# A hybrid decoder layer in fp32: where the DMAs that prepare a first sum of weights stand in the queue, and how they are laid out

## The chip, the cores and the metric

The kernel runs on one core of one Trainium2 chip. The metric is the device time of one execution in microseconds (us). Nothing else runs on the core's 16 DMA engines. Bytes that pass through HBM scratch cost nothing by themselves; only the time of the whole execution counts.

## The reference

One layer works on 256 tokens of width 4096, all in float32:

```
u     = rmsnorm(x) * norm_gain
proj  = u @ w_in                       # 4096 -> 16384: q k v z_a | h B C z_c
attn  = causal attention of 16 heads x 128, T5 bias, times silu(z_a)
conv  = B * short_conv(C * h) * silu(z_c)
out   = rmsnorm(x + concat(attn, conv) @ w_out) * final_gain     # 4096 -> 4096
```

With 256 tokens there is one attention block, so the block selection selects nothing and plain causal attention is left. Nearly all work is in the two projections: 4096x16384 and 4096x4096 weights, read once each, against 256 tokens.

## The kernel before

**Products.** TensorE multiplies in fp32r, which keeps less than fp32. So each operand is split in two, a rounded part `hi` and the rest `lo`, and a product is three matmuls: token-hi by weight-hi (line 644), token-lo by weight-hi (L645) and token-hi by weight-lo (L647). Each matmul is 128x128 by 128x512.

**Quads.** The weights are worked off in 320 *quads*. A quad holds 2 row blocks of 128 by 2 column blocks of 512 of a weight matrix, as one 128x2048 array (1 MB). Sixteen quads are one *pass*: a pair of column blocks over all 4096 rows. There are 16 passes of the input projection (`w`) and 4 of the output projection (`wout`). A quad is multiplied with the two token halves in one of two ways. A plain quad (P) takes eight products, 24 matmuls. A *seven* (S) takes Strassen's scheme in Winograd's form, seven products, 21 matmuls; it needs sums of its four weight blocks first. A string such as `"PSPSSPSSPSSPSSPP"` (`PATS`) fixes the order of P and S in a pass.

**Work on a quad's weights.** `load(n)` fetches quad n into one of three SBUF buffers `raw` (`AHEAD + 1`); it is called two quads ahead. `split(u)` then makes the operands. For a seven, VectorE (DVE) makes three blocks `sum`: one from `raw` (L552) and two more at once (L553). ScalarE (ACT) rounds `hi` (L570), VectorE subtracts for `lo` (L572). `hi` and `lo` have three buffers each (`RING`), and a seven takes two of them in turn, one for its four raw blocks and one for its three sums. A raw buffer is free when the last `lo` of its quad has been made, and the load of the quad three further on can then be issued.

**The first sum.** The first of a seven's sums, of blocks 12 and 11 of the quad, is not made on VectorE but by DMA, for the 150 sevens from pass 2 on (the list `PRE`). `first_sum(n)` copies block 12 of quad n (256 KB, the first 512 columns of the 128x2048 array) from HBM to a scratch place in HBM, with a DMA on the queue of SyncE (SP, L493), and then adds the second 512 columns to it by an accumulating DMA on the queue of GpSimd (POOL, L494). When the quad is loaded, its first 512 columns come from the scratch place (L515) and the other 1536 from the weights (L516). A quad outside `PRE` is loaded by one DMA (L518). The scratch is one tile of four places (`T1S`), used in turn. `load(n)` calls `first_sum` for a later seven, as long as fewer than three first sums are ahead, so that the k-th seven's load is written together with the copy for seven k+3.

**Order.** Each engine and each queue works off its instructions strictly in order, and the SP queue holds the raw loads, the copies, and small transfers (attention bias, intermediate results, tokens). A framework builds the order: it takes the kernel as written, works out which instruction depends on which, and may place an instruction that depends on less ahead of one that was written earlier. So the copies of `first_sum` need not stand where `load` writes them. An instruction at the head of a queue that waits holds up everything behind it. The copy for a place in scratch must wait until the last read of that place (an L515) has landed.

Of the kernel before, what the change touches and what calls it, by code (L numbers as in the profile page):

```python
# [10 lines left out]
F32 = mybir.dt.float32  # L11
# [3 lines left out]
ALU = mybir.AluOpType  # L15
AX = mybir.AxisListType

P = 128
# [3 lines left out]
NQ = KT // 2  # L22
# [6 lines left out]
B = 512  # L29
QUAD = 4 * B  # L30
WARM = 10
PRE_FROM = 2
T1S = 4
T1_AT = 26
AHEAD = 2

# [32 lines left out]
N_PAIRS = 16  # L69
# [11 lines left out]
def of(pattern):  # L81
    n = pattern.count("S")
    return in_order(pattern, SEVEN[:n], EIGHT + SEVEN[n:]), set(SEVEN[:n])
# [3 lines left out]
ORDERS, SEVENS = zip(*([(FIRST0, {8, 10, 12, 14}), (SECOND, {4, 6, 8, 10, 12, 14})]  # L87
                       + [of(PATS[k]) for k in KIND[2:N_PAIRS]]
                       + [(FIRST, {8, 10, 12, 14})] + [of(PATS[k]) for k in KIND[N_PAIRS + 1:]]))

BOTH = {q for q in range(NQ) for a, b in ((0, N_PAIRS), (N_PAIRS, N_PAIRS + NDP)) for p in range(a, b)
        if q in SEVENS[p] and any(q not in SEVENS[x] for x in range(p, b))}
SIZES = [8 if q in BOTH else 7 if any(q in x for x in SEVENS) else 4 for q in range(NQ)]

RAISE = {(1, 1): 4, (1, 3): 6, (1, 6): 0, (1, 8): 2, (1, 10): 11,
         (N_PAIRS, 6): 0, (N_PAIRS, 8): 2, (N_PAIRS, 10): 4, (N_PAIRS, 12): 6}
# [7 lines left out]
def hymba_layer(ctx: ExitStack, tc: tile.TileContext, xT, xres, gain, w, convw, wout,  # L104
                relb, onehot, fgain, out):
    nc = tc.nc
    PSUM = bass.MemoryType.PSUM
    ps_ = ctx.enter_context(tc.tile_pool(name="ps", bufs=1, space=PSUM))
    dram = ctx.enter_context(tc.tile_pool(name="dram", bufs=1, space=bass.MemoryType.DRAM))
# [42 lines left out]
    def operands(q):  # L152
        A[q] = kt.tile([P, SIZES[q], 2, P], F32R, name=f"k{q}")
        return A[q]

    def sums_of(q, c):

        for dst, a, b, op in ((4, 0, 2, ALU.add), (5, 4, 1, ALU.subtract),
                              (6, 3, 5, ALU.subtract), (g_at(q), 0, 1, ALU.subtract)):
            nc.vector.tensor_tensor(c[:, dst], c[:, a], c[:, b], op)  # L160

    def parts(dst, c):
        nc.scalar.copy(dst[:, :, 0], c)  # L163
        nc.vector.tensor_tensor(dst[:, :, 1], c, dst[:, :, 0].bitcast(F32), ALU.subtract)  # L164

    def x_load(q):
        xr = pool.tile([P, 2, S], F32, name="xr", tag="pt", bufs=4)
        nc.sync.dma_start(xr, xT[q].rearrange("p (k t) -> p k t", k=2))
        return xr
# [8 lines left out]
    def x_parts(q, xr):  # L178
        dst = operands(q)
        if q in SEVENS[0]:  # L180
            c = x_scaled(q, xr)
            sums_of(q, c)
            parts(dst, c[:, :SIZES[q]])
            return
# [12 lines left out]
    def m_parts(q, c):  # L197
        dst = operands(q)
        if q in SEVENS[N_PAIRS]:
            sums_of(q, c)  # L200
            parts(dst, c[:, :SIZES[q]])
        else:
# [275 lines left out]
            nc.sync.dma_start(out[t * P:(t + 1) * P, a:b], row)  # L478


    quads = [(p, i, q) for p, order in enumerate(ORDERS) for i, q in enumerate(order)]
    raws, xrs, halves, sums, kept_at = {}, {}, {}, {}, []

    PRE = [n for n, (p, i, q) in enumerate(quads) if q in SEVENS[p] and p >= PRE_FROM]
    t1_d = dram.tile([T1S, P, B], F32, name="t1_d")
    t1s, t1_next = {}, [0]

    def source(n):
        return w[n] if n < w.shape[0] else wout[n - w.shape[0]]

    def first_sum(n):
        t1 = t1s[n] = t1_d[PRE.index(n) % T1S]
        nc.sync.dma_start(t1, source(n)[:, :B])  # L493
        nc.gpsimd.dma_start(t1, source(n)[:, B:2 * B], accum_op=ALU.add)  # L494

    def load(n):
        if n >= len(quads):
            return
        p, i, q = quads[n]
        raw = raws[n] = wp.tile([P, QUAD], F32, name="raw", bufs=AHEAD + 1)  # L500
        src = source(n)
        if p == 0:
            if i == 0:
                nc.scalar.dma_start(g_sb, gain)
                xr = xrs[q] = pool.tile([P, 2, S], F32, name="xr", tag="pt", bufs=4)
                nc.scalar.dma_start(xr[:, 1], xT[q][:, S:])
            else:
                xrs[q] = x_load(q)
        if n < LEAD:
            for j in range(4):  # L510
                nc.sync.dma_start(raw[:, j * B:(j + 1) * B], src[:, j * B:(j + 1) * B])
                if n == 0 and j == 0:
                    nc.sync.dma_start(xrs[q][:, 0], xT[q][:, :S])
        elif n in PRE:
            nc.sync.dma_start(raw[:, :B], t1s.pop(n))  # L515
            nc.sync.dma_start(raw[:, B:], src[:, B:])  # L516
        else:
            nc.sync.dma_start(raw, src)  # L518
        if n >= T1_AT and len(t1s) < T1S - 1 and t1_next[0] < len(PRE):
            first_sum(PRE[t1_next[0]])  # L520
            t1_next[0] += 1


# [12 lines left out]
    def split(u):  # L536
# [4 lines left out]
        if first:  # L541
            load(n + AHEAD)
            if p == 0:
                x_parts(q, xrs.pop(q))
            if q in SEVENS[p]:
                raw = raws[n].rearrange("p (b c) -> p b c", b=4)

                k = sum(x in SEVENS[p] for x in ORDERS[p][:i])
                t = sums[n] = (cur["pool"] if k % 2 and p < N_PAIRS else wp).tile([P, 3, B], F32, name="sum")
                if n not in PRE:  # L550
                    nc.vector.tensor_tensor(raw[:, 0], raw[:, 0], raw[:, 1], ALU.add)
                nc.vector.tensor_tensor(t[:, 0], raw[:, 0], raw[:, 2], ALU.subtract)  # L552
                nc.vector.tensor_tensor(t[:, 1:], raw[:, 1::2], t[:, :1].to_broadcast([P, 2, B]), ALU.subtract)  # L553
# [3 lines left out]
        if p == N_PAIRS + NDP - 1 and i >= KEPT:  # L557

            spot = ORDERS[p][2 * len(kept_at):]
            kept_at.append(u)  # L560
            hi, lo = (kt.tile([P, SIZES[k], 2, P], F32R, name=f"k{k}")
                      .rearrange("p n h c -> p (n h c)") for k in spot[:2])
# [60 lines left out]
    for n in range(AHEAD):  # L623
        load(n)
# [25 lines left out]
    for u, (n, kind, at, products) in enumerate(units):  # L650
        p, i, q = quads[n]
# [16 lines left out]
        g = AHEAD_HI if len(products) > 2 and not late else 1  # L668
# [43 lines left out]
        if (p, i + 1) in RAISE:  # L712
            q = RAISE[p, i + 1]
            raised[q] = x_load(q) if p < N_PAIRS else m_load(q)
        if (p, i) in RAISE:
            q = RAISE[p, i]
# [21 lines left out]


def _layout(x, norm_gain, w_in, conv_w, w_out, rel_bias, final_gain):  # L740
    def blocks(src, order, c1, c2):

        b1, b2 = src[:, :, c1:c1 + B], src[:, :, c2:c2 + B]
        return [np.concatenate((b2[2 * q], b1[2 * q], b2[2 * q + 1], b1[2 * q + 1]), axis=1) for q in order]

    w = w_in[0].reshape(KT, P, 4 * 4096)
    w_quads = []
    for p, ((c1, c2), g) in enumerate(PAIRS):
        w_quads += blocks(w, ORDERS[p], c1 * 2048 + g * B, c2 * 2048 + g * B)
    w_quads = np.stack(w_quads)  # L750
    wo = w_out[0].reshape(KT, P, D)
    wo_quads = []
    for p in range(NDP):
        wo_quads += blocks(wo, ORDERS[N_PAIRS + p], 2 * p * B, (2 * p + 1) * B)
    wo_quads = np.stack(wo_quads)

    dist = 255 - np.arange(384)
    bucket = np.where(dist < 0, BUCKETS,
                      np.where(dist < 16, dist, 15 + np.searchsorted(EDGES, dist, side="right")))
    onehot = (bucket[None, :] == np.arange(BUCKETS + 1)[:, None]).astype(np.float32)  # L760
    return {
        "xT": x[0].T.reshape(NQ, 2, P, S).transpose(0, 2, 1, 3).reshape(NQ, P, 2 * S),
        "xres": x[0].reshape(2, P, NDP, 2 * B).transpose(2, 1, 0, 3).reshape(NDP, P, 4 * B),
        "gain": norm_gain[0].reshape(KT, P).T,
        "w": w_quads,
        "convw": conv_w[0].reshape(3, 16, P).transpose(2, 1, 0),
        "wout": wo_quads,
        "relb": rel_bias,
        "onehot": onehot,
        "fgain": final_gain,  # L770
    }
# [22 lines left out]
```

## Time and profile before

| | |
|---|---|
| median of 3 runs | 1818.78 us (1814.21 to 1820.96) |
| profiled execution | 1825.3 us, of which the span of the profile is 1823.5 us |
| TensorE busy in the profile | 1727.6 us, 95% of the span |
| VectorE busy | 1502.6 us, 82% |
| ScalarE busy | 1049.6 us, 58% |
| mean granted TensorE clock | 0.980 |
| moved by DMA | 449.21 MB, 246 GB/s over the span |

Busy times count an instruction from its start to its modelled end, and matmuls overlap each other: one is shown as 396 ns long, though in an undisturbed stretch they start every 0.227 us. So a busy share of TensorE of 95% does not say that 5% is all that is lost. A row of the timeline gives start, duration, engine, line, operation and what it writes and reads; a "q" behind the engine's name (SPq) means its queue, and the time of a DMA's row there is only that of issuing it. Brackets behind a row hold how long the engine had been idle and what it had waited for.

### The profile page before, as it was taken

To read this page: it belongs to the slowest core of one execution; us is meant where nothing else is said; L and a number is where in the kernel's file an instruction comes from. 1 tells how busy PE (TensorE), PEld (TensorE's weight loads), DVE (VectorE), ACT (ScalarE), POOL (GpSimd) and SP (SyncE) were. 2 spreads that over 40 slices of the span, in tenths; PEclk is the share of its full clock that TensorE was granted. 3 is DMA by queue.
4 is the path that set the end of the run, shared out by engine and by line. 5 is a ranking of instruction groups with operands and counts; after the bars stand their busy time and mean duration, and the time that the engine had idled before them with its cause. 6 is when DMAs were issued, how large, how long until landed. Compare 5 with 4: busy or idle time off the path is not lost.

```text
span 1823.5 us, 20698 instructions
## 1 busy us (share of the span) xinstructions
PE 1727.6 (95%) x7580; PEld 1408.4 (77%) x7580; DVE 1502.6 (82%) x1286; ACT 1049.6 (58%) x1161; POOL 124.2 (7%) x156
## 2 busy tenths in 40 slices
PE   9999999999999998989999999999999999999997
PEld 7888777777778777868777887787778777778776
DVE  6989787878797878878797978887889877878787
ACT  6867655665566555655465555555555645555453
POOL 0000100010000000000000000000000000000000
PEclk9999999999999999999999999999999999999998
DMA  9877877888787878687888888878888879787864
GB/s 335 282 264 246 238 255 225 254 239 257 205 271 220 261 216 263 178 247 231 240 258 251 259 244 241 272 209 254 232 268 237 285 262 300 233 256 225 249 222 168
DMA packets 131505, 449.21 MB, mean 246 GB/s; under 512 B 16171, under 2 KB 21068, under 8 KB 109900
## 3 DMA queue, kind: packets, MB, share of 16 engines
q1 hardware_dynamic: 109516, 408.42, 64.3%
q0 software_dynamic: 21600, 39.33, 15.3%
q8 instruction: 59, 0.97, 0.2%
q14 instruction: 42, 0.34, 0.1%
q10 hardware_dynamic: 288, 0.15, 0.0%
HBM read 438.66 MB, written 87.82 MB: 289 GB/s over the span
## 4 chain that ended last, share of the span: by engine, by line
PE 42%; DMA 28%; DVE 19%; issue 8%; ACT 2%; SPq 1%; DVEq 0%; ACTq 0%
DMA raw<-in_w_dram 17%; PE p L647 14%; PE p L645 13%; PE p L644 13%; DVE lo L572 13%; DMA raw<-in_wout_dram 6%; DMA raw<-t_d 2%; DVE sum L552 2%; ACT hi L570 2%; DVE sum L553 1%; DMA m_d<-mt 1%; SPq L515 1%; DMA c<-m_d 1%; PE p L283 0%; DMA xr<-in_xT_dram 0%
## 5 line engine op out<-in xcount | busy, mean ns | idle before, releaser
L644 PE MATMUL p<-hi,k 128*128 128x512 f32 x2376 | 937.1, 396 | 10.9 <-DVE es L375 4.1
L645 PE MATMUL p<-hi,k 128*128 128x512 f32 x2376 | 935.3, 395 | 0.1
L570 ACT CAST hi<-raw 128x1024 fp32r<-128x1024 f32 (+1 forms) x638 | 638.0, 1044 | 442.6 <-PE p L645 256.7
L572 DVE TENSOR_TENSOR lo<-raw,hi 128x2048 fp32r<-128x2048 f32 (+1 forms) x323 | 723.5, 2247 | 73.4 <-ACT hi L570 72.7
L647 PE MATMUL p<-lo,k 128*128 128x512 f32 x2376 | 648.0, 396 | 66.1 <-DVE lo L572 66.0
L647 PEld LDWEIGHTS p<-lo,k 128*128 128x128 f32 x2376 | 443.3, 189 | 169.0 <-DVE lo L572 82.1
L644 PEld LDWEIGHTS p<-hi,k 128*128 128x128 f32 x2376 | 454.2, 191 | 111.2 <-ACT hi L570 8.3
L645 PEld LDWEIGHTS p<-hi,k 128*128 128x128 f32 x2376 | 453.4, 191 | 96.9 <-issue 0.6
L570 ACT CAST hi<-sum 128x1536 fp32r<-128x1536 f32 x160 | 237.0, 1482 | 218.1 <-PE p L645 90.2
L572 DVE TENSOR_TENSOR lo<-sum,hi 128x1536 fp32r<-128x1536 f32 x160 | 280.3, 1752 | 9.6 <-ACT hi L570 8.8
L552 DVE TENSOR_TENSOR sum<-raw 128x512 f32<-128x512 f32 x160 | 110.1, 688 | 197.6 <-DMA raw<-in_w_dram 156.3
L553 DVE TENSOR_TENSOR sum<-raw,sum 128x1024 f32<-128x1024 f32 x160 | 195.5, 1222 | 2.7
L494 POOL DMA_DIRECT2D t_d<-in_w_dram x125 | 103.0, 830 | 1289.7 <-DMA t_d<-in_w_dram 1288.3
L382 ACT ACTIVATE es<-es,rT 128x512 f32<-128x512 f32 x56 | 38.3, 718 | 26.2 <-DVE es L376 20.9
L494 POOL DMA_DIRECT2D t_d<-in_wout_dram x25 | 20.5, 820 | 336.4 <-DMA t_d<-in_wout_dram 336.4
L163 ACT CAST k<-c 128x512 fp32r<-128x512 f32 (+4 forms) x38 | 21.8, 591 | 35.6 <-DVE c L160 24.4
L164 DVE TENSOR_TENSOR k<-c,k 128x512 fp32r<-128x512 f32 (+4 forms) x38 | 24.0, 650 | 0.7 <-ACT k L163 0.6
L160 DVE TENSOR_TENSOR c<-c 128x128 f32<-128x128 f32 x68 | 17.0, 286 | 9.0 <-DMA c<-m_d 7.9
L376 DVE TENSOR_TENSOR es<-p,es 128x1024 f32<-128x1024 f32 x20 | 24.3, 1217 | 0.0
L291 ACT ACTIVATE lg<-lg,st 128x256 f32<-128x256 f32 (+1 forms) x32 | 14.3, 447 | 6.2 <-DVE st L290 6.2
L283 PE MATMUL p<-qk 128*128 128x256 f32 x32 | 11.2, 436 | 4.9 <-ACT qk L278 4.0
L361 DVE SCALAR_TENSOR_TENSOR y<-p,cw,y 128x255 f32<-128x255 f32 (+1 forms) x32 | 14.1, 474 | 0.1
(107 smaller groups left out, 479.5 us busy)
## 6 DMA issues: line engine op xcount, KB each, us to landing
raw<-in_w_dram SPq DMA_DIRECT2D x129, 1024.0 KB, 7.1
raw<-in_w_dram SPq DMA_DIRECT2D x125, 768.0 KB, 6.9
raw<-in_wout_dram SPq DMA_DIRECT2D x39, 1024.0 KB, 7.4
raw<-t_d SPq DMA_DIRECT2D x150, 256.0 KB, 5.2
t_d<-in_w_dram SPq DMA_DIRECT2D x125, 256.0 KB, 5.3
t_d<-in_w_dram POOLq DMA_DIRECT2D x125, 256.0 KB, 7.1
raw<-in_wout_dram SPq DMA_DIRECT2D x25, 768.0 KB, 6.2
t_d<-in_wout_dram SPq DMA_DIRECT2D x25, 256.0 KB, 5.7
```

The costliest lines, as they stand in the source:

```text
L163: nc.scalar.copy(dst[:, :, 0], c)
L164: nc.vector.tensor_tensor(dst[:, :, 1], c, dst[:, :, 0].bitcast(F32), ALU.subtract)
L376: nc.vector.tensor_tensor(es[:, 1::2], acc[5][:, None, :].to_broadcast([P, 2, B]), es[:, 1:3], ALU.subtract)
L382: nc.scalar.activation(e, e, AF.Copy, scale=r)
L494: nc.gpsimd.dma_start(t1, source(n)[:, B:2 * B], accum_op=ALU.add)
L552: nc.vector.tensor_tensor(t[:, 0], raw[:, 0], raw[:, 2], ALU.subtract)
L553: nc.vector.tensor_tensor(t[:, 1:], raw[:, 1::2], t[:, :1].to_broadcast([P, 2, B]), ALU.subtract)
L570: nc.scalar.copy(hi[:, b:b + half], src[:, b:b + half])
L572: nc.vector.tensor_tensor(lo[:, c], src[:, c], hi[:, c].bitcast(F32), ALU.subtract)
L644: nc.tensor.matmul(acc[b_], a, h_, start=s0, stop=False)
L645: nc.tensor.matmul(acc[b_], b, h_, start=False, stop=False)
L647: nc.tensor.matmul(acc[b_], a, l_, start=False, stop=s1)
```

## The change

The change has four parts.

- The scratch has eight places instead of four, each a tile of its own. The number of first sums in the making stays at three (`T1_LEAD`).
- The call of `first_sum` in `load` is wrapped so that its SP instruction, the copy, must stand in the SP queue behind the last DMA of the raw load that it is written with.
- For the 150 sevens of `PRE`, the host lays out block 12 as 256 KB in one piece, and behind it the other three blocks as 128 rows of 6 KB. Before, all four were 128 rows of 8 KB. Bytes, and the shapes in SBUF, are the same.
- The copy of block 12 is now from one contiguous region to another, written as 32 pieces of 8 KB (`COPY`). The built instruction has 16 rows of 16 KB. Before it had 128 rows of 2 KB. The accumulating DMA and the load from scratch still go by 128 rows of 2 KB.

What is computed, on which engine, and the number of DMAs stay as they were.

```
-T1S = 4
+T1S = 8
+T1_LEAD = 3
+COPY = 32
...
+QUADS = [(p, i, q) for p, order in enumerate(ORDERS) for i, q in enumerate(order)]
+
+PRE = [n for n, (p, i, q) in enumerate(QUADS) if q in SEVENS[p] and p >= PRE_FROM]
...
-    t1_d = dram.tile([T1S, P, B], F32, name="t1_d")
+    t1_d = [dram.tile([COPY, P * B // COPY], F32, name=f"t1_{j}") for j in range(T1S)]
     t1s, t1_next = {}, [0]
...
+    def parted(n):
+
+        flat = source(n).rearrange("p c -> (p c)")
+        return flat[:P * B].rearrange("(a c) -> a c", a=COPY), flat[P * B:].rearrange("(p c) -> p c", p=P)
+
+    def by_rows(t1):
+        return t1.rearrange("a (r c) -> (a r) c", c=B)
+
     def first_sum(n):
         t1 = t1s[n] = t1_d[PRE.index(n) % T1S]
-        nc.sync.dma_start(t1, source(n)[:, :B])
-        nc.gpsimd.dma_start(t1, source(n)[:, B:2 * B], accum_op=ALU.add)
+        b12, rest = parted(n)
+        nc.sync.dma_start(t1, b12)
+        nc.gpsimd.dma_start(by_rows(t1), rest[:, :B], accum_op=ALU.add)
...
         elif n in PRE:
-            nc.sync.dma_start(raw[:, :B], t1s.pop(n))
-            nc.sync.dma_start(raw[:, B:], src[:, B:])
+            nc.sync.dma_start(raw[:, :B], by_rows(t1s.pop(n)))
+            last = nc.sync.dma_start(raw[:, B:], parted(n)[1])
         else:
-            nc.sync.dma_start(raw, src)
-        if n >= T1_AT and len(t1s) < T1S - 1 and t1_next[0] < len(PRE):
-            first_sum(PRE[t1_next[0]])
+            last = nc.sync.dma_start(raw, src)
+        if n >= T1_AT and len(t1s) < T1_LEAD and t1_next[0] < len(PRE):
+
+            with tc.issue_after(last.ins):
+                first_sum(PRE[t1_next[0]])
             t1_next[0] += 1
...
-        return [np.concatenate((b2[2 * q], b1[2 * q], b2[2 * q + 1], b1[2 * q + 1]), axis=1) for q in order]
+        made = []
+        for i, q in enumerate(ORDERS[p]):
+            first, rest = b2[2 * q], np.concatenate((b1[2 * q], b2[2 * q + 1], b1[2 * q + 1]), axis=1)
+            if NQ * p + i in PRE:
+                made.append(np.concatenate((first.reshape(-1), rest.reshape(-1))).reshape(P, QUAD))
+            else:
+                made.append(np.concatenate((first, rest), axis=1))
+        return made
```

How this moves the SP queue shows at two places. The first is in pass 2, where the order of the copies first departs from the written one. In these rows `raw<-t_d` (L515) and `raw<-in_w_dram` with 1536 columns (L516) are a seven's load, `raw<-in_w_dram` with 2048 columns (L518) is a plain quad's, and `t_d<-in_w_dram` (L493) is a copy. Before, two sevens, a plain quad and two sevens:

```order
L515 DMA raw<-t_d 128x512
L516 DMA raw<-in_w_dram 128x1536
L493 DMA t_d<-in_w_dram 128x512
L518 DMA raw<-in_w_dram 128x2048
L493 DMA t_d<-in_w_dram 128x512
L515 DMA raw<-t_d 128x512
L516 DMA raw<-in_w_dram 128x1536
L493 DMA t_d<-in_w_dram 128x512
L515 DMA raw<-t_d 128x512
L516 DMA raw<-in_w_dram 128x1536
L493 DMA t_d<-in_w_dram 128x512
```

The same place with the change; the lines are now L527 and L528 for a seven's load, L530 for a plain quad's and L505 for the copy, and the places in scratch are `t_0` to `t_7`:

```order
L527 DMA raw<-t_4_108 128x512
L528 DMA raw<-in_w_dram 128x1536
L505 DMA t_7_111<-in_w_dram 16x4096
L530 DMA raw<-in_w_dram 128x2048
L527 DMA raw<-t_5_109 128x512
L528 DMA raw<-in_w_dram 128x1536
L505 DMA t_0_104<-in_w_dram 16x4096
L527 DMA raw<-t_6_110 128x512
L528 DMA raw<-in_w_dram 128x1536
L505 DMA t_1_105<-in_w_dram 16x4096
```

Before, a second copy stands between the plain quad's load and the seven's load that it is written with. From there on the queue before is one copy ahead: what follows the load of seven k is the copy for seven k+4, and its place, k+4 modulo 4, is the very place that the load of seven k has just begun to read. With the change the copy that follows the load of seven k is for seven k+3, and its place was last read by the load of seven k-5.

The second place is where pass 2 ends and pass 3 begins. Before, three plain loads in a row, then two sevens' loads with a plain one between them:

```order
L518 DMA raw<-in_w_dram 128x2048 x3
L515 DMA raw<-t_d 128x512
L516 DMA raw<-in_w_dram 128x1536
L518 DMA raw<-in_w_dram 128x2048
L515 DMA raw<-t_d 128x512
L516 DMA raw<-in_w_dram 128x1536
L493 DMA t_d<-in_w_dram 128x512 x2
L515 DMA raw<-t_d 128x512
```

With the change:

```order
L530 DMA raw<-in_w_dram 128x2048 x3
L527 DMA raw<-t_1_105 128x512
L528 DMA raw<-in_w_dram 128x1536
L505 DMA t_4_108<-in_w_dram 16x4096
L530 DMA raw<-in_w_dram 128x2048
L527 DMA raw<-t_2_106 128x512
L528 DMA raw<-in_w_dram 128x1536
L505 DMA t_5_109<-in_w_dram 16x4096
```

Here two copies stood together ahead of a seven's load; now each stands behind a load, the first of them ahead of a plain quad's load instead. The order on GpSimd's queue, one accumulating DMA behind the other, is unchanged.

More of the change, by code (lines that the diff above doesn't have):

```diff
@@ L478, in finish @@
             nc.sync.dma_start(out[t * P:(t + 1) * P, a:b], row)
-    quads = [(p, i, q) for p, order in enumerate(ORDERS) for i, q in enumerate(order)]
+    quads = QUADS
     raws, xrs, halves, sums, kept_at = {}, {}, {}, {}, []
-    PRE = [n for n, (p, i, q) in enumerate(quads) if q in SEVENS[p] and p >= PRE_FROM]
-    t1_d = dram.tile([T1S, P, B], F32, name="t1_d")
+    t1_d = [dram.tile([COPY, P * B // COPY], F32, name=f"t1_{j}") for j in range(T1S)]
     t1s, t1_next = {}, [0]
@@ L740, in _layout, with blocks @@
 def _layout(x, norm_gain, w_in, conv_w, w_out, rel_bias, final_gain):
-    def blocks(src, order, c1, c2):
+    def blocks(src, p, c1, c2):
         b1, b2 = src[:, :, c1:c1 + B], src[:, :, c2:c2 + B]
-        return [np.concatenate((b2[2 * q], b1[2 * q], b2[2 * q + 1], b1[2 * q + 1]), axis=1) for q in order]
+        made = []
[6 more added lines that the diff above has]
+        return made
     w = w_in[0].reshape(KT, P, 4 * 4096)
@@ L748, in _layout @@
     for p, ((c1, c2), g) in enumerate(PAIRS):
-        w_quads += blocks(w, ORDERS[p], c1 * 2048 + g * B, c2 * 2048 + g * B)
+        w_quads += blocks(w, p, c1 * 2048 + g * B, c2 * 2048 + g * B)
     w_quads = np.stack(w_quads)
@@ L753, in _layout @@
     for p in range(NDP):
-        wo_quads += blocks(wo, ORDERS[N_PAIRS + p], 2 * p * B, (2 * p + 1) * B)
+        wo_quads += blocks(wo, N_PAIRS + p, 2 * p * B, (2 * p + 1) * B)
     wo_quads = np.stack(wo_quads)
```

## The prediction

> **What bounds the kernel now.** First the page: the span, busy times, DMA, and the chain that ended last.
>
> ```profile
> span 1823.5 us, 20698 instructions
> PE 1727.6 (95%) x7580; PEld 1408.4 (77%) x7580; DVE 1502.6 (82%) x1286; ACT 1049.6 (58%) x1161; POOL 124.2 (7%) x156
> DMA  9877877888787878687888888878888879787864
> q1 hardware_dynamic: 109516, 408.42, 64.3%
> q0 software_dynamic: 21600, 39.33, 15.3%
> PE 42%; DMA 28%; DVE 19%; issue 8%; ACT 2%; SPq 1%; DVEq 0%; ACTq 0%
> DMA raw<-in_w_dram 17%; PE p L647 14%; PE p L645 13%; PE p L644 13%; DVE lo L572 13%; DMA raw<-in_wout_dram 6%; DMA raw<-t_d 2%; DVE sum L552 2%; ACT hi L570 2%; DVE sum L553 1%; DMA m_d<-mt 1%; SPq L515 1%; DMA c<-m_d 1%; PE p L283 0%; DMA xr<-in_xT_dram 0%
> ```
>
> TensorE is the bound, but the chain spends 28% in DMA and 19% in VectorE: now and then a raw load is late, VectorE with it, and TensorE waits. The DMA engines are 80% busy all along, so a transfer queues behind others. Next the waits, of the engines and of the SP queue:
>
> ```profile
> PE p L647 <- DVE lo L572: 66.0, 36, 4.8
> DVE sum L552 <- DMA raw<-in_w_dram: 156.3, 53, 7.2
> SPq L493 <- DMA raw<-t_d: 490.4, 121, 8.9
> ```
>
> TensorE's largest wait is for `lo`, 66.0 us in 36 waits, 1.31 us in the first and 0.31 in the last:
>
> ```profile
> 222.98 0.96 PE L647 MATMUL p<-lo,k 128*128 128x512 f32 x3 [1.31 <-DVE lo L572]
> 1792.61 0.73 PE L647 MATMUL p<-lo,k 128*128 128x512 f32 x2 [0.31 <-DVE lo L572]
> ```
>
> The SP queue stands 490.4 us at the copy (L493), 4.1 us each, until the load of the seven ahead of it has read its place. One such stretch, SP first:
>
> ```profile
> 659.35 0.32 SPq L515 DMA_DIRECT2D raw<-t_d  x1
> 659.72 0.68 SPq L516 DMA_DIRECT2D raw<-in_w_dram  x1
> 664.98 0.50 SPq L493 DMA_DIRECT2D t_d<-in_w_dram  x1
> 665.64 0.47 SPq L515 DMA_DIRECT2D raw<-t_d  x1
> 666.15 0.43 SPq L516 DMA_DIRECT2D raw<-in_w_dram  x1
> 670.80 0.50 SPq L493 DMA_DIRECT2D t_d<-in_w_dram  x1
> 672.80 0.33 SPq L518 DMA_DIRECT2D raw<-in_w_dram  x1
> 675.70 0.33 SPq L515 DMA_DIRECT2D raw<-t_d  x1
> 676.07 0.59 SPq L516 DMA_DIRECT2D raw<-in_w_dram  x1
> ```
>
> Then VectorE and TensorE:
>
> ```profile
> 660.91 2.29 DVE L572 TENSOR_TENSOR lo<-raw,hi 128x2048 fp32r<-128x2048 f32 x1
> 673.39 2.28 DVE L572 TENSOR_TENSOR lo<-raw,hi 128x2048 fp32r<-128x2048 f32 x1
> 683.77 0.69 DVE L552 TENSOR_TENSOR sum<-raw 128x512 f32<-128x512 f32 x1 [3.09 <-DMA raw<-in_w_dram]
> 687.45 0.73 PE L647 MATMUL p<-lo,k 128*128 128x512 f32 x2 [1.57 <-DVE lo L572]
> ```
>
> The copy at 664.98 waited 4.6 us behind the load of 659.72. The buffer for the next seven had been free since 663.20 (660.91 + 2.29), but its load stood behind the copy and went out at 665.64, 2.4 us late. The copy of 670.80 then lies ahead of the plain quad's load (672.80) and the third seven's (675.70), and all share 16 DMA engines. That third seven lands near 683.7, 8 us after issue; VectorE idles 3.09 us for it, and TensorE 1.57.
>
> **The change part by part.** *The copy moves behind the raw load.* Its engine time is in no row. Below, a transfer of the mean rate of q1: 64.3% of 1823.5 us is 1172 us for 408.42 MB, 2.87 us per MB, 0.75 us for the copy's 0.262 MB. Above, an accumulating DMA of the same size: 15.3% of 1823.5 is 279 us, by 150 it is 1.86 us. A copy goes from HBM to HBM as that does but needs no addition; I take the middle, 1.3 us. Of the 36 waits for `lo`, 33 (63.0 us) follow a load at which, or at the one before which, a copy had been issued and not landed, as in the stretch above. If that copy has run earlier, behind the seven before, the load lands up to 1.3 us sooner, and each wait shrinks by that or by what it has: over the 33, by 35 us (21 at 0.75, 45 at 1.86).
>
> *The stall at the copy goes.* With eight places the copy's place was last read five sevens earlier, and SP stands there no longer. Of the 490.4 us most covers itself, since the next raw buffer isn't free yet. I compared each raw load behind a copy with the `lo` that frees its buffer: 44 loads went out over 0.5 us late, 111.5 us in all, 2.5 each. First and last of them, with the copy ahead:
>
> ```profile
> 218.60 0.50 SPq L493 DMA_DIRECT2D t_d<-in_w_dram  x1
> 219.22 0.51 SPq L515 DMA_DIRECT2D raw<-t_d  x1
> 1744.55 0.50 SPq L493 DMA_DIRECT2D t_d<-in_wout_dram  x1
> 1745.14 0.54 SPq L518 DMA_DIRECT2D raw<-in_wout_dram  x1
> ```
>
> Such a load often had slack. In the stretch above, the `lo` of 670.49 held VectorE until 672.8, so landing sooner would have started nothing sooner. Bounds are 0, and the 47 us of the 22 waits that have a late load among the four up to them. I take 8: the chain gives `raw<-t_d` 2%, half a dozen pieces, and a late load costs 2.5, which makes 15, half of it given back where another chain takes over.
>
> *The clock.* After long waits TensorE runs slowly for a while:
>
> ```profile
> 785.78 1.65 PE L647 MATMUL p<-lo,k 128*128 128x512 f32 x3 [4.80 <-DVE lo L572]
> 787.23 0.63 PE L644 MATMUL p<-hi,k 128*128 128x512 f32 x1
> 790.20 0.40 PE L645 MATMUL p<-hi,k 128*128 128x512 f32 x1
> 1158.43 0.92 PE L647 MATMUL p<-lo,k 128*128 128x512 f32 x2 [2.06 <-DVE lo L572]
> ```
>
> ```profile
> 783.35:790.18 6.83, 4.40 (x10) 3.47 (x11) 6.12 (x5) 2.23 (x2) 0.81 (x1) 0.50 0.70 194
> ```
>
> From 783.35 to 790.18 the granted clock is 0.50: 7 matmuls take 2.97 us there (787.23 to 790.20), 0.42 each, against 0.227. With those of the row before, such a stretch costs 1.5 to 2 us beyond its wait; I take 1.8. Thirteen of the 36 waits are over 2 us, 11 of them with such a stretch, the shortest 2.06 (1158.43). Less 1.3, eight of the 13 fall under 2, six with a stretch: 6 x 1.8 = 11 us (0 if the waits stay, 20 if all go). The Trainium skill (TensorE: Matmul & The Clock Gate, Part 1 and the rules at the end) puts the loss down to idle windows of about 3.4 us and asks for no gaps over about 3; the row of 2.06 us shows a shorter one to be enough. By the page's 3 us only six of the waits would cost a stretch, and less 1.3 four of them fall under it: 4 x 1.8 = 7 us in place of 11, an estimate from that page.
>
> *Large pieces, block 12 by itself.* A copy moves the same 0.262 MB with fewer, larger pieces; behind a load it is covered by the 5 us to the next one. At best its engine time falls from 1.3 to 0.75, which shortens nothing that is waited for; I take 0, and between -5 and +5. The 6 KB rows of the rest are as long as before.
>
> *What the new place costs.* In 45 of 150 sevens the next raw buffer comes free within 3.5 us of the seven's load; then the copy is ahead of that load, 1.3 us x 45 = 59 us of lateness. Late loads before were 111.5 us and, beside crowding, gave 66 of waits: at half a us per us this is up to 29. But these next loads are plain quads in 31 of 45, which make no sum and whose `lo` has most time; and before, most had a copy ahead too. I take 10 us.
>
> The sum: 35 + 8 + 11 + 0 - 10 = 44 us off the profiled execution's 1823.5 (its own time is 1825.3, 6.5 above the median of the runs). Some will come back at `lo` itself, since two sevens in a row give VectorE 2 x 5.95 us (0.69 + 1.22 + 2.29 + 1.75) for 2 x 4.77 us of TensorE (21 matmuls of 0.227). I take 40: 1818.8 - 40 = **1779 us**.
>
> That a load isn't hurt by the copy right behind it, the trace shows: 16 sevens have it so already. First and last:
>
> ```profile
> 190.25 0.39 SPq L516 DMA_DIRECT2D raw<-in_w_dram  x1
> 190.71 0.50 SPq L493 DMA_DIRECT2D t_d<-in_w_dram  x1
> 1362.44 0.42 SPq L516 DMA_DIRECT2D raw<-in_w_dram  x1
> 1362.92 0.50 SPq L493 DMA_DIRECT2D t_d<-in_w_dram  x1
> ```
>
> ```profile
> DMA to landing us min/median/max: 4.4/4.4/4.4
> DMA to landing us min/median/max: 5.1/5.1/5.1
> DMA to landing us min/median/max: 4.2/6.8/12.5
> ```
>
> The rows are the landing of the first, of the last, and of all L516. The 16 average 5.6 us, the others 7.1; several stand in quiet stretches, so the 1.5 us between is no pure effect.
>
> **The rivals.** *Nothing:* the DMA engines are the limit, and a copy moved is a load delayed elsewhere. For it speaks 80% of busy time. Against it: the 20% that is left lies just where SP stands at the copy. It gives 1812 to 1826.
>
> *All of it:* every wait for `lo` goes with its stretch, 66 + 20 = 86 us: 1733. Against it stand VectorE's 5.95 us for a seven; 1733 to 1752 with some left.
>
> *Slower:* the copy, now beside every seven's load and ahead of 45 following ones, makes the loads land later. It decides if a load with a copy close behind lands over 0.75 us later than now. Then 43 to 45 loads with no slack pay 0.75 each to TensorE and nothing is won: 1818.8 + 32 = 1851. Against it: the 4.4 and 5.1 us above. The Trainium skill (DMA: Bandwidth & Descriptors, Latency and other measured facts) has HBM access rise from 0.2 us to 2 under high load, which would speak for it, as more is in flight at once; by its 1.8 us, an estimate, 45 loads would cost 81 us. No row here has shown that.
>
> *The change doesn't do what it says:* the copy still waits, for another semaphore. The order puts no reader of its place near it. It would give 1819 and is counted under nothing.
>
> **How the numbers follow.** Forecast 0.56 (1752 to 1806), nothing 0.18, all 0.14, slower 0.12. Within 0.5%, 9 us, a measurement of this kernel tells nothing from no change. So faster is 0.56 + 0.14 = 0.70, same 0.18, slower 0.12. The range takes in most of the forecast and of nothing, and a part of all: 1746 to 1820.
>
> **What would show it.** SP's wait at the copy for `raw<-t` should fall from 490 us to nearly 0, and raw loads late by it from 44 to a few. `PE p <- DVE lo` should fall from 66.0 to about 30, L516's median landing from 6.8 to about 6, and the mean clock rise from 0.98. If SP's wait goes and the wait for `lo` stays above 55, the DMA engines were the limit. If the landing of sevens rises above 7, the slower case is at work. If waits of SP at the load from scratch for the accumulating DMA appear, the first sums have become too late, which the three sevens of lead should rule out.

## The result, and the profile after

The changed kernel takes **1704.0 us**, median of 3 runs (1702.77 to 1704.12), against 1818.78 before: a ratio of 0.937, 95% interval 0.934 to 0.940. The forecast was 1779. Faster was right; the gain of 115 us is nearly three times the 40 that were forecast, and beyond the end of the range at 1746.

First the page of the changed kernel: the span, busy times, TensorE and DMA by slices, the two large queues (packets, MB, share of 16 engines' time) and the chain that ended last by engine.

```profile
span 1702.2 us, 20691 instructions
PE 1686.7 (99%) x7580; PEld 1391.8 (82%) x7580; DVE 1506.8 (89%) x1286; ACT 1047.5 (62%) x1161; POOL 123.9 (7%) x156
...
PE   9999999999999999999999999999999999999997
...
DMA  8878879878887888787888888878888888888764
...
q1 hardware_dynamic: 92716, 408.42, 66.9%
q0 software_dynamic: 21600, 39.33, 14.8%
...
PE 95%; ACT 1%; DVE 1%; issue 1%; DMA 1%; DVEq 0%; SPq 0%; ACTq 0%
```

The chain of waits is now TensorE for 95%; DMA and VectorE, 28% and 19% of it before, have 1% each. The span is 121.3 us shorter. Of that, 80.4 us are time in which TensorE stood still (span less busy time: 95.9 before, 15.5 after). The other 40.9 are busy time itself, 1727.6 to 1686.7 for the same 7580 matmuls: at half the granted clock a matmul counts as busy for longer. The mean granted clock went from 0.980 to 0.998. Matmuls that follow the one before at 0.38 to 0.48 us, where 0.227 is usual, fell from 127 to 11, which is 23 us. The other 18 us are not accounted for.

Next the groups of instructions (busy us, mean ns | idle time before them and what ended most of it) and the landing times (KB, median us from issue to landing):

```profile
L661 PE MATMUL p<-lo,k 128*128 128x512 f32 x2376 | 637.3, 392 | 0.0
...
L566 DVE TENSOR_TENSOR sum<-raw 128x512 f32<-128x512 f32 x160 | 109.7, 685 | 40.9 <-DMA raw<-in_w_dram 23.7
...
raw<-in_w_dram SPq DMA_DIRECT2D x125, 768.0 KB, 6.1
...
raw<-t SPq DMA_DIRECT2D x150, 256.0 KB, 4.0
...
t<-in_w_dram POOLq DMA_DIRECT2D x125, 256.0 KB, 5.6
```

TensorE waits 0.0 us at the matmuls by `lo`, 66.0 before. VectorE's wait for the raw load is 23.7 us, 156.3 before. The accumulating transfers land in 5.6 us (7.1 before), the loads from scratch in 4.0 (5.2). Last the waits of the SP queue:

```profile
SPq L530 <- DVE lo L586: 550.2, 147, 8.0
SPq L527 <- DVE lo L586: 482.7, 115, 9.6
SPq L527 <- DVE sum L567: 46.1, 13, 4.7
```

The 490.4 us at the copy are gone. SP now waits at the loads themselves, for a free raw buffer. This costs nothing by itself: no load can go out before its buffer is free.

### The profile page after: what moved, and what is told of

Its sections match the earlier page's. It is cut to its first block, busy times and chain, and to the rows that moved or that the text cites. A ratio compares the mean times of both kernels' runs of the same rounds, so it can differ in the third digit from the quotient of the medians.

```text
span 1702.2 us, 20691 instructions
## 1 busy us (share of the span) xinstructions
PE 1686.7 (99%) x7580; PEld 1391.8 (82%) x7580; DVE 1506.8 (89%) x1286; ACT 1047.5 (62%) x1161; POOL 123.9 (7%) x156
## 3 DMA queue, kind: packets, MB, share of 16 engines
q1 hardware_dynamic: 92716, 408.42, 66.9%
q0 software_dynamic: 21600, 39.33, 14.8%
## 4 chain that ended last, share of the span: by engine, by line
PE 95%; ACT 1%; DVE 1%; issue 1%; DMA 1%; DVEq 0%; SPq 0%; ACTq 0%
PE p L659 31%; PE p L658 31%; PE p L661 31%; DMA raw<-in_w_dram 1%; ACT hi L584 0%; PE p L281 0%; DVE lo L586 0%; PE p L305 0%; PE p L288 0%; ACT L296 0%; ACT L401 0%; DVE es L381 0%; PE p L314 0%; PE p L316 0%; PE p L315 0%
## 5 line engine op out<-in xcount | busy, mean ns | idle before, releaser
L658 PE MATMUL p<-hi,k 128*128 128x512 f32 x2376 | 923.9, 390 | 2.7 <-DVE es L381 1.3
L659 PE MATMUL p<-hi,k 128*128 128x512 f32 x2376 | 923.8, 390 | 0.1
L661 PE MATMUL p<-lo,k 128*128 128x512 f32 x2376 | 637.3, 392 | 0.0
L658 PEld LDWEIGHTS p<-hi,k 128*128 128x128 f32 x2376 | 446.1, 188 | 97.5 <-issue 2.5
L659 PEld LDWEIGHTS p<-hi,k 128*128 128x128 f32 x2376 | 445.9, 188 | 93.4 <-issue 0.6
L506 POOL DMA_DIRECT2D t<-in_w_dram x125 | 102.7, 822 | 1205.3 <-DMA t<-in_w_dram 924.4
L566 DVE TENSOR_TENSOR sum<-raw 128x512 f32<-128x512 f32 x160 | 109.7, 685 | 40.9 <-DMA raw<-in_w_dram 23.7
L506 POOL DMA_DIRECT2D t<-in_wout_dram x25 | 20.5, 819 | 306.0 <-DMA t<-in_wout_dram 219.9
L379 DVE TENSOR_TENSOR es<-p,es 128x512 f32<-128x512 f32 x20 | 13.7, 687 | 16.3 <-PE p L661 16.2
L378 ACT COPY es<-p 128x512 f32<-128x512 f32 x20 | 11.6, 582 | 20.5 <-PE p L661 20.5
L283 ACT COPY qk<-p 128x512 f32<-128x512 f32 x16 | 9.3, 582 | 10.3 <-PE p L281 10.2
```

Source lines behind the costliest of these rows:

```text
L506: nc.gpsimd.dma_start(by_rows(t1), rest[:, :B], accum_op=ALU.add)
L658: nc.tensor.matmul(acc[b_], a, h_, start=s0, stop=False)
L659: nc.tensor.matmul(acc[b_], b, h_, start=False, stop=False)
L661: nc.tensor.matmul(acc[b_], a, l_, start=False, stop=s1)
```

## The experiments

Ratios below are to the kernel before, run beside each kernel on the same chip; the kernel before had medians of 1813.1 to 1821.1 us there. Two theories stood at the start. *Stall:* the copies' place in the queue makes the loads late, as the prediction had it. *Crowding:* the transfers themselves are too slow, and the layout makes them cheaper.

**Parts of the change alone.** Eight places, nothing else:

```
-T1S = 4
+T1S = 8
+T1_LEAD = 3
-        if n >= T1_AT and len(t1s) < T1S - 1 and ...
+        if n >= T1_AT and len(t1s) < T1_LEAD and ...
```

> Eight places alone; order free, rows as before. In the built order the copy now runs eight sevens ahead instead of four (114 of 150), so it again writes the place that the load just ahead of it has begun to read. Stall theory (the SP queue standing at the copy is what made loads late): SP still waits about 490 us at L493 and the time stays at 1810 to 1825. Theory that the number of places is what counts: the stall goes and the time falls to about 1704.

Measured: 1832.46 us, ratio 1.007 (1.003 to 1.011). With eight places the framework runs the copies up to eight sevens ahead (114 of 150), and the copy waits for its place as before. Places without the queue order do not help; the time is 0.7% longer, if anything. The waits of SP and of TensorE:

```profile
SPq L494 <- DMA raw<-t_d: 477.7, 115, 9.5
...
PE p L648 <- DVE lo L573: 65.7, 31, 6.0
```

Only the queue order, on the old layout and four places:

```
-            nc.sync.dma_start(raw[:, B:], src[:, B:])
+            last = nc.sync.dma_start(raw[:, B:], src[:, B:])
...
-            first_sum(PRE[t1_next[0]])
+            with tc.issue_after(last.ins):
+                first_sum(PRE[t1_next[0]])
```

> Only the order: the copy for seven k+3 behind the load of seven k, four places, rows as before. Its place was last read by the load of seven k-1, one seven earlier. Stall theory: SP's wait at the copy falls from 490 us to under 60 and the time to 1704 to 1725. Crowding theory (the DMA engines' time for the copies is what made loads late, so the large pieces count): the time stays above 1760.

Measured: 1769.85 us, 0.972 (0.968 to 0.976). The waits:

```profile
SPq L493 <- DMA raw<-t_d: 12.2, 20, 1.3
...
PE p L648 <- DVE lo L573: 39.1, 27, 2.8
```

SP's stall is gone, 12.2 us left of 490.4, and the wait for `lo` is 39.1. The forecast's mechanism works, and at the forecast's size: 49 us. It isn't the whole. Both parts together, still on the old layout (the two diffs above):

> Order and eight places, block 12 in 128 rows of 2 KB as before. Stall theory: within 5 us of the whole change, 1704 to 1709. Crowding theory: copies of 1.3 us engine time instead of about 0.6 leave part of the waits for lo, 1740 to 1790.

Measured: 1762.21 us, 0.968 (0.963 to 0.973), 8 us less than with four places, with intervals that overlap. The wait for `lo` is 36.2 us. VectorE and ScalarE wait 107.8 and 44.0 us for raw loads of `w`, 151.8 together; before it was 156.3 and 85.6, together 241.9:

```profile
PE p L649 <- DVE lo L574: 36.2, 26, 3.3
...
DVE sum L554 <- DMA raw<-in_w_dram: 107.8, 47, 4.7
...
ACT hi L572 <- DMA raw<-in_w_dram: 44.0, 42, 2.9
```

Then the other half, the layout and the large pieces, with four places and copies where the framework puts them. The diff is against the changed kernel:

```
-T1S = 8
+T1S = 4
...
-            with tc.issue_after(last.ins):
-                first_sum(PRE[t1_next[0]])
+            first_sum(PRE[t1_next[0]])
```

> Only the layout and the large pieces, four places, order free. In the built order the copy is for seven k+3 in 92 places and for k+4 in 56. Stall theory: the stall stays at the 56 places, about 56/119 of it; the time falls by about half, 1750 to 1790. Crowding theory: cheaper copies alone give most of the gain, under 1740.

Measured: 1705.29 us, 0.936 (0.932 to 0.940), nearly the whole gain. SP's queue still waits at the copy:

```profile
SPq L505 <- DMA raw<-t: 82.7, 33, 5.0
```

So a kernel with 12.2 us of this wait takes 1770 and one with 82.7 takes 1705. The sum of the waits at the copy does not set the time.

**Pieces and rows.** The next four took the layout apart. First block 12 in 128 pieces of 2 KB again, out of an extra input `b12` with gaps between the pieces, all else as changed:

```
-COPY = 32
+COPY = 128
+PAD = 128
...
-        nc.sync.dma_start(t1, b12)
+        nc.sync.dma_start(t1, b12[PRE.index(n)][:, :P * B // COPY])
```

> The whole change, but block 12 is copied as 128 rows of 2 KB (from an input array of its own with a gap behind each row); the other blocks lie as in the change. Pieces theory (many short pieces of the copy make loads late): 1755 to 1775, as without the layout. Layout theory (the 6 KB step of the rest, instead of 8 KB, makes loads and accumulating DMAs faster): 1704 to 1712.

Measured: 1719.33 us, 0.945 (0.939 to 0.950). Now block 12 in large pieces out of the extra input, and the other three blocks left where they were, in rows of 6 KB that lie 8 KB apart:

```
-        return flat[:P * B].rearrange("(a c) -> a c", a=COPY), flat[P * B:].rearrange("(p c) -> p c", p=P)
+        return None, source(n)[:, B:]
...
-            if NQ * p + i in PRE:
+            if False:
```

> The whole change, with block 12 copied in 16 rows of 16 KB from an input array of its own, and the other blocks at steps of 8 KB as before. Pieces theory: 1704 to 1712. Layout theory: 1755 to 1775.

Measured: 1759.81 us, 0.967 (0.960 to 0.973). Then 32 pieces of 8 KB, with gaps (`PAD = 512`, `COPY = 32`):

> The whole change with block 12 in 32 rows of 8 KB. Pieces theory: 1704 to 1715, since most of the cut from 128 to 16 pieces is there. Layout theory: 1704, as the layout is the change's.

Measured: 1704.16 us, 0.936 (0.931 to 0.941). Then the changed kernel with a second copy of each block 12 to a place that nobody reads:

```
+        nc.sync.dma_start(t1_x[PRE.index(n) % T1S], b12)
```

> The whole change, and each block 12 copied a second time, in large pieces, to a place nobody reads: twice the bytes and engine time of the copies. If the DMA engines' busy time is what counts, the copy now takes 1.3 us as it did before, and the time goes back to 1750 or more. If it is the number of short pieces and not the bytes, the time stays under 1720.

Measured: 1761.16 us, 0.968 (0.962 to 0.973). Taken at their word, the old row step (1759.81) and the doubled copy (1761.16) say that the rows' step and the time on the DMA engines are each worth some 57 us. But what TensorE waited for was new; its waits with the old row step:

```profile
PE p L658 <- ACT hi L584: 19.8, 12, 4.1
PE p L661 <- DVE lo L586: 3.2, 5, 1.6
```

A DMA that is changed should not turn a wait for `lo` into one for `hi`. The order of the built instructions shows why it did: a transfer with another shape moves instructions on *every* engine, it seems because the framework places them by its own idea of when their inputs are there. Against the kernel before, the changed one has 524 of VectorE's 1286 places filled otherwise, 245 of ScalarE's 1100 and 531 of TensorE's 7499. The two kernels of 1760 share one order of TensorE and almost one of the other two, unlike both. The queue order alone, both parts on the old layout, and the 2 KB pieces share an order too, one near that of before (75, 45 and 138 places). Every comparison above therefore mixes two things, except between kernels of one order. The 8 KB pieces have the order of the changed kernel on all engines, and its time. Both parts on the old layout (1762.21) and the 2 KB pieces (1719.33) have one order too, on SP as well, and give 43 us for the layout alone.

**The engines' order held.** From here on the order is written into the kernel, as a table of places and edges between neighbours on one engine, which order and don't wait:

```
+def pin(tc, nc):
+    for engine, moved in PINNED.items():
+        traced = [i for i in nc.cur_bb.bb.instructions
+                  if str(i.engine) == f"EngineType.{engine}" and type(i).__name__.startswith("Inst")]
+        order = list(range(len(traced)))
+        for at, places in moved.items():
+            order[at:at + len(places)] = places
+        for a, b in zip(order, order[1:]):
+            tc.add_manual_dep(traced[b], traced[a].name,
+                              mybir.DependencyInfo(mybir.DependencyClass.NoSync, mybir.DependencyReason.DATA),
+                              reason="pin")
```

The kernel before, transfers untouched, with the changed kernel's order on TensorE, VectorE and ScalarE:

> The kernel before with nothing of the change in it, but with the instructions of TensorE, VectorE and ScalarE held to the order in which the changed kernel has them (edges that only order, no waits; the framework had put 524 of VectorE's 1286 places, 245 of ScalarE's 1100 and 531 of TensorE's 7499 otherwise in the two kernels). If this order carries the gain: 1705 to 1745 us and the waits of TensorE for lo mostly gone. If the transfers carry it, 1795 to 1825 us: the split runs against the small pieces at an order much like before's showed 43 of the 115 us from the layout, and at most 15 us for order and piece size together.

Measured: 1772.63 us, 0.976 (0.970 to 0.982). Some 40 us (32 to 55 by the interval) come from the order alone, and the wait for `lo` falls to a quarter. SP was left free here: in the trace 82 of its 841 transfers stand otherwise than before. The waits of TensorE, ScalarE and VectorE:

```profile
PE p L647 <- DVE lo L572: 16.4, 19, 2.2
PE p L355 <- DVE es L375: 12.7, 3, 4.4
PE p L644 <- DVE es L375: 11.6, 3, 4.3
...
ACT hi L570 <- DMA raw<-in_w_dram: 157.3, 98, 3.7
...
DVE sum L552 <- DMA raw<-in_w_dram: 66.2, 27, 5.1
```

The reverse, the changed kernel at the order of before:

> The changed kernel, all its transfers, with the three engines held to the order of the kernel before. If the transfers carry the gain: 1704 to 1725 us. If the engines' order carries it: 1775 to 1815 us. If both are needed, between them, with waits of TensorE for lo over 10 us.

Measured: 1761.53 us, 0.971 (0.966 to 0.977). It looks as if half were lost. The waits of TensorE, and one of four equal stretches (SP, VectorE, TensorE), say where:

```profile
PE p L658 <- DVE lg L291: 29.4, 4, 8.3
PE p L661 <- DVE lo L586: 3.1, 3, 1.6
```

```profile
173.23 8.32 SPq L272 DMA_DIRECT2D bt<-bias_d  x16
...
181.66 0.36 SPq L527 DMA_DIRECT2D raw<-t  x1
...
186.53 0.69 DVE L566 TENSOR_TENSOR sum<-raw 128x512 f32<-128x512 f32 x1 [7.75 <-DMA raw<-in_w_dram]
...
188.93 0.55 DVE L291 TENSOR_TENSOR lg<-p,bt 128x384 f32<-128x384 f32 x1
...
189.54 0.80 PE L658 MATMUL p<-hi,k 128*128 128x512 f32 x1 [7.38 <-DVE lg L291]
```

Sixteen small loads of the bias table hold SP's queue for 8.32 us ahead of a seven's load. VectorE's order, from the other kernel, has that seven's sum ahead of the `lg` that TensorE needs, so VectorE idles 7.75 us and TensorE 7.38. In the changed kernel the same sixteen loads stand there and harm nothing, since its VectorE has the `lg` first. Holding three engines and leaving the queue free had made a mismatch of its own; the waits for `lo`, 3.1 us, were gone even at the old order.

The old row step at the changed kernel's order:

> The run with the old 8 KB step for the three blocks left (its 1759.81 us was at an order of the engines of its own), now held to the changed kernel's order. If the row step makes the accumulating transfers slow and these set the time: 1740 to 1765 us again, accumulates landing in over 7 us. If its 56 us came from the other order: 1704 to 1720 us, though the accumulates still land in over 7 us.

Measured: 1725.22 us, 0.952 (0.946 to 0.958). Of the 56 us over the changed kernel, 35 were the order; 21 stay, with SP left free. The 2 KB pieces at that order:

> The run with 128 pieces of 2 KB for block 12 (1719.33 us at an order close to before's), now held to the changed kernel's order. If its 15 us over the changed kernel were the order: 1703 to 1709 us. If they were the piece size: 1715 to 1723 us.

Measured: 1703.68 us, 0.939 (0.934 to 0.944). The size of the pieces makes no difference; the 15 us were the order.

**SP held too.** The changed kernel at the order of before, with SP also as before except that each copy stands behind its raw load:

> The changed kernel with TensorE, VectorE and ScalarE at the order of the kernel before, as in the run before this one of that kind, but now SyncE too keeps the order of the kernel before, except that each copy stands behind its raw load. In the earlier run 29.4 us were four TensorE waits for lg, where SyncE issued sixteen small loads of the bias table ahead of a raw load that VectorE's order wanted first. If that mismatch was what was missing and the transfers carry most of the gain: 1705 to 1735 us, no lg waits. If the engines' order is worth as much as the transfers: 1750 to 1775 us.

Measured: 1712.84 us, 0.942 (0.939 to 0.945). The transfers alone, with the copies behind the loads in SP's queue and all else at the old order, give 107 us beside 1819.7 for the kernel before. The page, and TensorE's largest wait:

```profile
span 1710.6 us, 20717 instructions
...
PE 1691.0 (99%) x7580; PEld 1392.8 (81%) x7580; DVE 1503.6 (88%) x1286; ACT 1049.5 (61%) x1161; POOL 124.1 (7%) x156
```

```profile
PE p L661 <- DVE lo L586: 2.8, 2, 2.3
```

Old layout, all four engines as in the changed kernel:

> The old layout (block 12 in 2 KB pieces, all rows 8 KB apart) with eight places and the copies behind the raw loads, all four engines at exactly the changed kernel's order; at its own order it took 1762.21 us. If the layout is still needed at this order: 1720 to 1745 us, accumulates landing in about 7 us. If the order made the difference: 1704 to 1712 us.

Measured: 1717.85 us, 0.945 (0.941 to 0.948). Against the changed kernel that is 14 us for the layout at one order of all four, and it isn't the pieces. It points at the rows' step of 6 instead of 8 KB. The copy's own rows lie 8 KB apart here too, which was not tried alone; the queue that holds the copies takes no longer by it (66.3% of 1719.9 against 66.9% of 1702.2, 1140 and 1139 us). The queue of the accumulating DMAs does, and they land later. In this kernel, in the one with the old step and large pieces, and in the one with the new step and 2 KB pieces:

```profile
q0 software_dynamic: 21600, 39.33, 16.7%
...
t_d<-in_w_dram POOLq DMA_DIRECT2D x125, 256.0 KB, 6.8
```

```profile
q0 software_dynamic: 21600, 39.33, 16.5%
...
t<-in_w_dram POOLq DMA_DIRECT2D x125, 256.0 KB, 6.6
```

```profile
q0 software_dynamic: 21600, 39.33, 14.6%
...
t<-in_w_dram POOLq DMA_DIRECT2D x125, 256.0 KB, 5.6
```

That is 287 and 284 us of the engines' time (16.7% of 1719.9, 16.5% of 1722.8) with the old step, 249 with the new one (14.6% of 1704.0). The doubled copy at the changed kernel's order:

> The changed kernel with the second, unread copy of each block 12 (58 us more of the 16 DMA engines' time), now with all four engines at the changed kernel's order; at its own order it took 1761.16 us. If time on the DMA engines is what had to be freed: 1735 to 1765 us and waits for raw loads again. If the 57 us came from the other order: 1704 to 1715 us.

Measured: 1707.14 us, 0.939 (0.936 to 0.942). The queue's share:

```profile
q1 hardware_dynamic: 97516, 447.75, 71.8%
```

71.8% of 1704.5 is 1224 us against 1139 in the changed kernel: 85 us more of the DMA engines' time, for 3 us. The layout frees less of it, some 38 us (287 to 249), and is worth 14. So at this order crowding as a sum of engine time is out; the 54 us that it had seemed to cost were the order's.

**What in the order.** The kernel before has a pattern that explains its waits for `lo`. Rows of VectorE around its longest one:

```profile
772.59 2.28 DVE L572 TENSOR_TENSOR lo<-raw,hi 128x2048 fp32r<-128x2048 f32 x1
782.11 0.69 DVE L552 TENSOR_TENSOR sum<-raw 128x512 f32<-128x512 f32 x1 [7.23 <-DMA raw<-in_w_dram]
782.84 1.22 DVE L553 TENSOR_TENSOR sum<-raw,sum 128x1024 f32<-128x1024 f32 x1
783.98 1.75 DVE L572 TENSOR_TENSOR lo<-sum,hi 128x1536 fp32r<-128x1536 f32 x1
```

VectorE idles 7.23 us for the raw load of the *next* seven, and the `lo` of the seven in hand stands behind that, which TensorE gets 4.80 us late (the row of 785.78 in the prediction). The Trainium skill (PSUM — Partial Sum Buffer, Engine vs sequencer instructions) calls VectorE's queue strictly first in, first out; this stretch agrees. In the order before, 75 of 160 sevens have the next seven's sums ahead of their `lo`; in the changed one 14. Of the 36 waits for `lo`, 25 (53.6 of 66.0 us) follow such a `lo`. So these sums were moved behind the `lo`, and nothing else, first in the kernel before:

```
 order of VectorE, at 75 places
-sum<-raw          (next seven)
-sum<-raw,sum      (next seven)
 lo<-sum           (this seven)
+sum<-raw          (next seven)
+sum<-raw,sum      (next seven)
```

> The kernel before, its transfers and its order on every engine, but for one thing on VectorE: at the 75 sevens where the first sums of the next seven (which wait for its raw load) stood ahead of this seven's lo, they now stand right behind it. In the trace of before 25 of TensorE's 36 waits for lo, 53.6 of 66.0 us, follow such a lo. If this is what the other order is worth: 1765 to 1785 us, as with the whole order of the changed kernel (1772.63), TensorE's waits for lo below 30 us. If the order works by something else: 1805 to 1825 us.

Measured: 1808.19 us, 0.995 (0.992 to 0.999). Its waits of TensorE, ScalarE and VectorE:

```profile
PE p L647 <- DVE lo L572: 16.7, 14, 2.3
PE p L355 <- DVE es L375: 11.2, 3, 4.7
PE p L335 <- DVE am L314: 8.3, 4, 2.8
...
ACT hi L570 <- DMA raw<-in_w_dram: 148.6, 94, 4.0
...
DVE sum L552 <- DMA raw<-in_w_dram: 67.1, 30, 4.7
```

The named wait fell from 66.0 to 16.7, as with the whole order, yet only some 10 us of time came of it. VectorE's wait for the raw load is 89 us less, ScalarE's for the same loads 63 us more (85.6 before), and TensorE now stands at other things. The theory that this pattern was what the order is worth has fallen; the whole order of the changed kernel left those two waits much the same (66.2 and 157.3 us) and won 40 us. In the kernel with eight places and copies behind the loads, old layout:

> The same one move on VectorE (74 places) in the kernel with the old layout, eight places and the copies behind the raw loads, which took 1762.21 us at its own order and 1717.85 at the changed kernel's. If the move is what the order is worth: 1712 to 1735 us. If not: 1750 to 1770 us.

Measured: 1748.51 us, 0.962 (0.957 to 0.967): 14 of the 44 us between its own order and the changed kernel's, though the intervals of the two runs overlap (0.963 to 0.973 at its own order). And the 14 places left in the changed kernel:

> The changed kernel with the same move at the 14 places that its own order has left. TensorE stands still for 15.5 us of its span, most of it at the start and at the ends of passes, so little is left to win: 1700 to 1706 us if these places cost up to 3 us, and the same time within 0.1% if nothing waits at them any more.

Measured: 1708.8 us, 0.941 (0.937 to 0.945): no gain. It is 5 us over the changed kernel, above what was expected, with intervals that overlap.

All crosses in one table (median us; the ratios are above):

| transfers | engines at an order near that of before | at the changed kernel's |
|---|---|---|
| as before | 1818.78 | 1772.63 (SP free) |
| 8 places, copies behind loads, old layout | 1762.21 | 1717.85 |
| new layout, 4 places, copies as the framework puts them | not tried | 1705.29 (130 places of VectorE apart) |
| the whole change | 1712.84 | 1704.0 |

From here on *queue order* means the copies behind their loads together with the eight places. With the old layout the engines' order and the queue order add up: 40 and 57 us alone, 101 together. The layout is worth 67 us with the changed kernel's engine order alone, 43 to 49 with the queue order alone, and 14 with both. Once it is there, the queue order is worth 1 us and the engines' order 9. Near 1704 TensorE is 99% busy, and little is left to win.

Queue order and layout work alike. The waits of VectorE and ScalarE for raw loads of `w`, 241.9 us before, are 151.8 with the queue order, 74.1 (54.8 and 19.3) with the layout too at the old engine order, and 46.0 (23.7 and 22.3) in the changed kernel. The engines' order works otherwise: by itself it leaves 223.5 us of them, yet TensorE stands still for 62.1 us (1776.8 less 1714.7) in place of 95.9.

What stays open: which of the other differences in order bring the rest of its 40 us, and by which path the layout helps. The median landing isn't it: with the doubled copy the loads of sevens and the accumulates land as late as with the old layout (6.7 against 6.6 us and 6.8 against 6.8), and little is lost. The latest loads differ. The landing of the sevens' loads, and the chain that ended last, with the old layout and then with the doubled copy, both at the changed kernel's order:

```profile
DMA to landing us min/median/max: 4.2/6.6/11.0
...
PE 85%; DMA 6%; DVE 4%; issue 3%; ACT 2%; SPq 0%; DVEq 0%; ACTq 0%
```

```profile
DMA to landing us min/median/max: 4.1/6.7/9.4
...
PE 89%; DVE 3%; DMA 3%; issue 2%; ACT 2%; SPq 0%; DVEq 0%; ACTq 0%
```

The longest waits for raw loads in the chain are 10.10 us in the first and 7.21 in the second; in the run with the old step and large pieces (1725.22) one is 9.91. That the layout helps by sparing the latest loads is likely, and not shown.

## Why the prediction was right and wrong

- **Direction and mechanism of the queue order: right.** SP's wait at the copy went from 490.4 us to none, the wait for `lo` from 66.0 to 0 (about 30 forecast; 36.2 with the queue order alone), the landing of the sevens' loads from 6.9 to 6.1, the clock from 0.980 to 0.998. SP waits at the loads from scratch for the first sums for 2.5 us in two waits, and landing did not rise, so the slower case had nothing to stand on.
- **The copy behind the load (35), the stall (8), the clock (11), the new place (-10), together 44: too small, but near.** Alone they measured 57 us, and 49 with four places, at an order near that of before. The single sizes are not confirmed. The copy's engine time, taken as 1.3 us, came out at 0.57 in its new form (85 us for 150 more copies), below the lower bound of 0.75. And the stall that was priced by late loads is no measure of time: 82.7 us of it were left in a kernel of 1705.
- **Large pieces, block 12 by itself, "I take 0": the step that failed.** The large pieces are worth 0 indeed (1703.68 against 1704.0). But the step looked at the copy alone and dismissed the rest because its 6 KB rows "are as long as before". They lie closer, 6 KB apart and no longer 8, and the accumulating DMA reads them. At an order near that of before the layout is worth 43 us (1762.21 to 1719.33), at the changed kernel's 14. With 43 in its place the sum would have been 87, and the forecast 1732 us. The accumulating DMAs, which the prediction left as they were, are cheaper by it (249 us in place of 284 to 287); the path from there to the time stays open.
- **The order of VectorE, ScalarE and TensorE: not looked at.** The prediction compared the orders of SP and GpSimd, the queues on which the edit stands. The framework moved the other engines with them. With the transfers of before that is worth 40 us or so, with those of the change 9 (1712.84 to 1704.0). Beginning at the order of before, the 115 us are 57 for the queue order, 49 for the layout (1762.21 to 1712.84) and 9 for the order; the forecast had 40, 0 and 0.
- **Given back at `lo` (44 to 40): wrong.** VectorE's 5.95 us for a seven against TensorE's 4.77 held nothing back: VectorE is 89% busy and no wait for `lo` is left.
- **Rival "all of it": the right mechanism, too small a price.** 86 us counted the waits for `lo` and their slow stretches. Measured were 80.4 us of standing still, since the waits for other things went too, and 40.9 of busy time, of which about 23 were half-speed matmuls where 20 had been counted.
- **Rival "nothing", the DMA engines as the limit: refuted** by the 1704 us, against its 1812 to 1826, and in the changed kernel by 85 us of added transfers for 3 us.

## What to carry to other kernels

Where a framework orders the work, compare the order of every engine, not of the queue that was edited: a transfer with another shape can move instructions on all of them. Hold the order fixed on all engines, the DMA queue among them, before a part of a change is given its price; with three held and one free, or all free, five runs here were off by 15 to 54 us. A large wait that goes away is no gain yet: its cause, late loads here, may only queue up behind another engine, as ScalarE's 63 us did.

## What the runs showed of the hardware

An accumulating DMA of 128 pieces of 2 KB, HBM to HBM, is dearer when its source rows lie 8 KB apart than at 6 KB: the queue takes 284 to 287 us in place of 249 for the same 39.33 MB, and the landing in the three kernels shown is 6.6 to 6.8 us in place of 5.6. The 6 KB packets of the raw loads took no less: 264 ns in the mean, 247 before and 253 with the old layout at the changed kernel's order. The Trainium skill (DMA: Bandwidth & Descriptors, Latency and other measured facts) reports slower HBM copies where rows lie large powers of two apart: 207 GB/s at 512 KiB, the smallest it lists, and 164 at 2 MiB, against 214 with padded rows. The direction agrees with the 284 to 287 and 249 us here, but a step as small as 8 KB is not in it, and whether the cause is the same no run shows. A plain copy in HBM costs the same engine time in 2 KB pieces as in 16 KB ones, within what the queue's share can tell (67.2% of 1704.0 us against 66.9% of 1702.2, 6 us over 150 copies).
